# The down projection of a SwiGLU block as one level of Strassen for 18 of its 22 chunks

## The chip, the cores and the metric

The kernel runs on one core of a Trainium2 chip. The metric is device time in microseconds (us), from the start of an execution to its end on that core. The engines are named as the profile names them: PE (TensorE matmuls), PEld (TensorE weight loads), DVE (VectorE), ACT (ScalarE), POOL (GpSimd), and SP (SyncE, which here only issues DMAs). Each engine works through its own list of instructions in order, and waits on semaphores where it needs another engine's result.

## The reference

One transformer block on 1024 tokens of width 1024 in float32: sliding-window attention with sinks, then a SwiGLU feed-forward of inner width 2816 = 22 chunks of 128, then a final norm. The part that the change touches is the last product of the feed-forward:

```python
def swiglu_ffn(h, w_gate_up, w_down):
    gu = h @ w_gate_up
    return (jax.nn.silu(gu[..., :D_FF]) * gu[..., D_FF:]) @ w_down

x = x + mix
x = x + swiglu_ffn(rms_norm(x, norm_ffn), w_gate_up, w_down)
return rms_norm(x, final_norm)
```

## The kernel before

Every float32 operand of a large product is split into a high part (rounded to the matmul's type fp32r, made by ACT) and a low part (operand minus high part, made by DVE or POOL). A product is three matmuls per 128-deep step: high by high, high by low, low by high. All matmuls of the two last stages have 512 columns.

**Gate and up stage** (line 1022). Each of 22 column groups `g` is already done as one level of Strassen: seven products of 12 matmuls in the order 1, 6, 5, 7, 2, 4, 3, with weight sums made by POOL (tile `sum`, line 894), splits into `ws` (ACT line 914, DVE line 918), and evictions from the PSUM banks `gu_A` to `gu_D` on DVE and ACT. A pair of groups gives two chunks of the activation, `gate` times `up` (line 960 on POOL or 962 on DVE), and each finished chunk is stored to DRAM (`act_dram`, line 965).

**Down stage** (line 1219). The 22 chunks are taken in seven rounds of 3, 3, 4, 3, 3, 3, 3. In each round, for each of eight token tiles `t` and two column halves `nh`, PE accumulates the round's chunks in one PSUM bank `d`, and DVE adds the bank to the output tile `acc` in SBUF (line 1227). Activation chunks (`raw_a`) and rows of `w_down` (`raw_d`) come back from DRAM and are split by `d_steps` (ACT line 1122, DVE line 1126) into seven chunk slots of four tiles each; those in the tile `HH`, which held the normed tokens, and in `ws_d` and `dx` are slots of this kind.

The order of all work is written out by hand: `Q.put(n, step)` lets a step be issued after n more matmuls, so that the steps of the next round stand between the matmuls of this one on the other engines' lists.

```python
for t in range(NT):
    for nh in range(2):
        for c in cs:
            for a, b in ((0, 0), (0, 1), (1, 0)):
                nc.tensor.matmul(v4(ps), a_[:, a, t // 2], d_[:, b], ...)
                Q.tick()
        Q.put(4, add)      # acc[t][:, s] = ps + acc[t][:, s], on DVE
```

Of the kernel before, what the change touches and what calls it, by code (L numbers as in the profile page):

```python
# [26 lines left out]
NF = FF // P  # L27
# [5 lines left out]
def trunk_kernel(  # L33
# [13 lines left out]
    nc = tc.nc  # L47
# [47 lines left out]
    class Norm:  # L95
# [468 lines left out]
    def v4(ap):  # L564
        return ap.rearrange("p (k n) -> p k n", k=4)
# [204 lines left out]
    def add_raw_act(c):  # L770
        raw_jobs.append((("a", c), lambda raw: nc.sync.dma_start(raw, act_dram[c])))

    def add_raw_dn(c):
        raw_jobs.append((("d", c), lambda raw: nc.sync.dma_start(raw, w_dn[c * P : (c + 1) * P, :])))
# [330 lines left out]
    slots = {}

    def h_slot(par, k0):
        return [HH[:, j, :, k0 : k0 + 4, par * P : par * P + P] for j in range(4)]

    slots[1], slots[2], slots[4], slots[5] = h_slot(0, 0), h_slot(0, 4), h_slot(1, 0), h_slot(1, 4)  # L1110

    def d_steps(c, j):

        key = ("a" if j < 2 else "d", c)

        def src():
            return v4(raws[key][:, (j % 2) * 512 : (j % 2) * 512 + 512])
# [19 lines left out]
    def d_prep(left):
        for c, j in D_FIRST[left]:
            for i, st in enumerate(d_steps(c, j)):
                Q.put(1 + 3 * i, st)  # L1140
# [60 lines left out]
    c0 = 0  # L1201
    for r, size in enumerate(ROUNDS):
        cs = range(c0, c0 + size)
        c0 += size
        if r + 1 < len(ROUNDS):
            more = [st for c in range(c0, c0 + ROUNDS[r + 1]) for j in range(4) for st in d_steps(c, j)]
            for i, st in enumerate(more):
                Q.put(1 + i * (48 * size - 8) // len(more), st)
        for t in range(NT):
            for nh in range(2):  # L1210
                pool, tag = (psg, "g") if nh else (psa, "a")
                ps = pool.tile([P, 512], F32, tag=tag, name=f"d_{r}_{t}_{nh}")
                s = slice(nh * 512, nh * 512 + 512)
                n = 0
                for c in cs:
                    sl = slots[c % 7]
                    a_, d_ = sl[t % 2], sl[2 + nh]
                    for a, b in ((0, 0), (0, 1), (1, 0)):
                        nc.tensor.matmul(  # L1219
                            v4(ps), a_[:, a, t // 2], d_[:, b],  # L1220
                            start=(n == 0), stop=(n == 3 * size - 1),
                        )
                        n += 1
                        Q.tick()

                def add(r=r, t=t, nh=nh, s=s, ps=ps):
                    nc.vector.tensor_tensor(acc[t][:, s], ps, acc[t][:, s], ALU.add)  # L1227
                    if r == len(ROUNDS) - 1:
                        final_norm(t, nh)

                if t == NT - 1 and r == len(ROUNDS) - 1:
                    add()
                else:
                    Q.put(4, add)
# [30 lines left out]
```

## Time and profile before

| what | value |
|---|---|
| time, median of 3 runs | 1059.92 us (1058.37 to 1060.86) |
| time of the profiled execution | 1059.88 us |
| its span, first to last instruction | 1058.1 us, mean granted TensorE clock 0.985 |
| PE busy | 1026.3 us of the span, 97% |
| DVE, ACT, POOL busy | 609.3, 422.2 and 359.7 us |
| down stage, 808.6 to 1051.0 us | PE busy all of it, 1056 matmuls |

The profile is one execution. Its time is 0.04 us from the median, so that what is worked out from its rows can be set against either. Busy time says how much an engine did, not what the end waits for; for that the chain that ended last is read, and, for one stage, the windows and the waits.

### The profile page before, as it was taken

Reading aid. Unit: us, or ns where it says so; the run is one execution under the profiler, and the core shown is the slowest. Engines: PE = TensorE matmul, PEld = TensorE weight load, DVE = VectorE, ACT = ScalarE, POOL = GpSimd, SP = SyncE. Lnnn points to the kernel's source line nnn. Section 1 sums busy time; section 2 is a strip of 40 time slices with the busy share of each in tenths; the row PEclk is TensorE's granted clock in tenths of the full one; section 3 lists DMA queues with packets and bytes.
Section 4 is the critical chain, followed back from the end, with each engine's and each line's share of the span. In section 5 each row is a group of like instructions: output and inputs, shape, how many; then the busy total and the mean of one; then the engine's idle time right before and its main releaser. Section 6 shows DMA issues by size and latency. Waiting matters only on the chain.

```text
span 1058.1 us, 13677 instructions
## 1 busy us (share of the span) xinstructions
PE 1026.3 (97%) x4848; PEld 846.1 (80%) x4848; DVE 609.3 (58%) x1071; ACT 422.2 (40%) x893; POOL 359.7 (34%) x406
## 2 busy tenths in 40 slices
PE   7999999999987899999999999999999999999997
PEld 7888788888765698888888888888888888888885
DVE  5421687778885666454555455456446664455545
ACT  5432777777754443322332332232333212221115
POOL 4634555565334454163254154245131000000001
PEclk8999999999988899999999999999999999999999
DMA  8457555554546423132122132132126632233103
GB/s 276 127 132 204 138 160 146 154 179 130 141 125 190 132 80 100 60 106 73 60 100 99 41 120 77 44 120 80 42 99 237 239 121 80 80 100 99 42 20 139
DMA packets 92500, 124.11 MB, mean 117 GB/s; under 512 B 5648, under 2 KB 66064, under 8 KB 92432
## 3 DMA queue, kind: packets, MB, share of 16 engines
q1 hardware_dynamic: 92144, 122.45, 37.5%
q8 instruction: 38, 0.62, 0.2%
q10 hardware_dynamic: 288, 0.79, 0.2%
q14 instruction: 30, 0.25, 0.1%
HBM read 92.81 MB, written 28.31 MB: 114 GB/s over the span
## 4 chain that ended last, share of the span: by engine, by line
PE 64%; POOL 1%; ACT 1%; DVE 0%; issue 0%; POOLq 0%; ACTq 0%
PE d L1219 23%; PE gu_C L1022 12%; PE gu_B L1022 12%; PE gu_A L1022 12%; PE gu_D L1022 6%; PE mo L1035 1%; POOL sum L894 0%; POOL wc_oB L63 0%; POOL xr L636 0%; ACT acc L1197 0%; DVE ws L918 0%; PE pt_b L615 0%; ACT junk L1181 0%; ACT HT L616 0%; ACT sq L1174 0%
## 5 line engine op out<-in xcount | busy, mean ns | idle before, releaser
L1219 PE MATMUL d<-HH 128*128 128x512 f32 x576 | 150.6, 393 | 0.0
L1227 DVE TENSOR_TENSOR acc<-d,acc 128x512 f32<-128x512 f32 x112 | 77.3, 691 | 110.1 <-PE d L1219 103.8
L1022 PE MATMUL gu_A<-HH,ws 128*128 128x512 f32 (+2 forms) x552 | 132.2, 388 | 0.0
L960 POOL TENSOR_TENSOR gate<-gate,up 128x512 f32<-128x512 f32 x33 | 47.6, 1443 | 246.3 <-issue 195.0
L1219 PEld LDWEIGHTS d<-HH 128*128 128x128 f32 x576 | 108.3, 188 | 23.8
L246 PE MATMUL pc<-HH,wc_c 128*128 128x512 f32 x480 | 122.0, 398 | 0.0
L1022 PEld LDWEIGHTS gu_A<-HH,ws 128*128 128x128 f32 x552 | 101.7, 188 | 22.9
L918 DVE TENSOR_TENSOR ws<-sum,ws 128x512 fp32r<-128x512 f32 x88 | 85.9, 987 | 54.8 <-ACT ws L914 54.2
L246 PEld LDWEIGHTS pc<-HH,wc_c 128*128 128x128 f32 x480 | 87.4, 188 | 17.8
L914 ACT ACTIVATE ws<-raw_g 128x512 fp32r<-128x512 f32 x66 | 40.9, 630 | 140.0 <-issue 51.4
L1219 PE MATMUL d<-ws_d,ws_d 128*128 128x512 f32 x336 | 94.9, 391 | 0.0
L914 ACT ACTIVATE ws<-sum 128x512 fp32r<-128x512 f32 x88 | 54.0, 626 | 99.8 <-POOL sum L894 62.8
L1175 POOL TENSOR_SCALAR ssq_f<-ssq_f 128x1 f32<-128x1 f32 x7 | 1.3, 191 | 232.7 <-ACT sq L1174 232.7
L491 POOL TENSOR_SCALAR t<-t,st 128x256 f32<-128x256 f32 (+1 forms) x128 | 60.4, 491 | 52.8 <-DVE st L489 34.9
L1219 PEld LDWEIGHTS d<-ws_d,ws_d 128*128 128x128 f32 x336 | 63.0, 188 | 14.3
L478 ACT ACTIVATE t<-t,st 128x256 f32<-128x256 f32 (+1 forms) x128 | 61.9, 485 | 29.1 <-DVE st L470 29.1
L918 DVE TENSOR_TENSOR ws<-raw_g,ws 128x512 fp32r<-128x512 f32 x66 | 56.0, 857 | 29.7 <-ACT ws L914 28.8
L1022 PE MATMUL gu_C<-HT,ws 128*128 128x512 f32 (+2 forms) x288 | 67.6, 382 | 0.4 <-DVE ws L918 0.4
L979 DVE TENSOR_TENSOR u<-gu_B,p 128x512 f32<-128x512 f32 x44 | 30.3, 689 | 65.1 <-PE gu_B L1022 57.1
L1022 PE MATMUL gu_D<-HT,ws 128*128 128x512 f32 (+2 forms) x276 | 66.4, 389 | 0.0
L1022 PE MATMUL gu_B<-HT,ws 128*128 128x512 f32 (+2 forms) x276 | 65.9, 388 | 0.0
L1022 PE MATMUL gu_C<-HH,ws 128*128 128x512 f32 x264 | 65.2, 396 | 0.0
(165 smaller groups left out, 1871.9 us busy)
## 6 DMA issues: line engine op xcount, KB each, us to landing
raw_g<-in_ffn_w_gate_up_dram SPq DMA_DIRECT2D x44, 512.0 KB, 3.6
act<-gate SPq DMA_DIRECT2D x22, 512.0 KB, 2.6
raw_a<-act SPq DMA_DIRECT2D x22, 512.0 KB, 3.3
raw_d<-in_ffn_w_down_dram SPq DMA_DIRECT2D x22, 512.0 KB, 3.3
raw_c<-in_swa_w_in_dram SPq DMA_DIRECT2D x20, 512.0 KB, 4.0
qs<-qst SPq DMA_DIRECT2D x64, 128.0 KB, 2.5
qt<-qs SPq DMA_DIRECT2D x32, 256.0 KB, 4.6
x<-in_x_dram SPq DMA_DIRECT2D x8, 512.0 KB, 5.8
```

Of the source, the lines that this page charges most:

```text
L246: nc.tensor.matmul(ps, wc[:, wl, k], hh[:, :, hl, k, :], start=(n == 0), stop=(n == 3 * NK - 1))
L478: nc.scalar.activation(self.tt[:, g, b0:], self.tt[:, g, b0:], AF.Exp, bias=st[:, 0, g : g + 1], scale=-1.0, accum_out=st[:, 3, g : g + 1],)
L491: nc.gpsimd.tensor_scalar(self.tt[:, g, b0:], self.tt[:, g, b0:], st[:, 2, g : g + 1], 0.0, ALU.mult, ALU.add)
L914: nc.scalar.activation(w[:, 0], src(), AF.Copy)
L918: nc.vector.tensor_tensor(w[:, 1], src(), f(w[:, 0]), ALU.subtract)
L960: nc.gpsimd.tensor_tensor(gate[:, s], gate[:, s], ups[kp, f_][:, s], ALU.mult)
L979: nc.vector.tensor_tensor(us[g][:, n * 512 : n * 512 + 512], banks[g, "B"], p1s[g], ALU.add)
L1022: nc.tensor.matmul(v4(ps)[:, j0:j1], w[:, wl, k], moving(i, hl, k, j0, j1), start=(first and part != "l" and n == 0), stop=(n == 11), skip ...
L1035: nc.tensor.matmul(opss[2 * i + nh], o[:, a, c % G], wt[:, b, c % 2], start=(c == 0 and n == 0), stop=(c == 7 and n == 2),)
L1175: nc.gpsimd.tensor_scalar(st[:, 3:4], st[:, 0:1], 1.0 / D, EPS, ALU.mult, ALU.add)
L1219: nc.tensor.matmul(v4(ps), a_[:, a, t // 2], d_[:, b], start=(n == 0), stop=(n == 3 * size - 1),)
L1227: nc.vector.tensor_tensor(acc[t][:, s], ps, acc[t][:, s], ALU.add)
```

## The change

It replaces the down stage for 18 of the 22 chunks. Two neighbouring chunks of the activation (a pair `p`, nine pairs) times two column halves of `w_down`, with even and odd token tiles as the other split, are one 2 by 2 block product, and it is done with seven block products instead of eight. The nine pairs go in four rounds of 2, 2, 2 and 3 (`DROUNDS`). In a round, product `i` in the order 1, 2, 6, 7, 5, 3, 4 (`DORDER`) runs over `j` = 0 to 3 (each `j` is a pair of token tiles) and over the pairs, 3 matmuls each: 24 matmuls in a round of two pairs, 36 in the round of three. Products 1, 2 and then 5, 3 share the four banks X; 6, 7 and then 4 the four banks Y: product 2 adds on the banks of product 1 after product 1's own value was taken out, and likewise 7 on 6 and 3 on 5. The last four chunks are done as before, all at the end, 12 matmuls for each tile and half.

The left operands (sums of activations) are made in the gate and up stage by POOL, four for each pair (`act_sums`), and stored as three and a half tiles a pair in place of two. The right operands (differences of blocks of `w_down`) are made by POOL in the down stage, in `d_steps`, four for each pair: two for product 6, one for 7, one for 4. Both are split as before, the left ones (`s`) by ACT and POOL, the right ones (`w`) by ACT and DVE, into a ring of 16 slots, all in `HH`. Evictions stay on DVE, but for products 1 and 7 of the first round, which ACT copies. Four output tiles get their last sums on POOL (`y_sums`).

```diff
+    DROUNDS = (2, 2, 2, 3)
+        elif acts[kp, f_] == 2 and acts.get((kp, 1 - f_), 0) == 2:
+            act_sums(kp)
...
+            (u1[:, a], g0[:, b], g1[:, b], ALU.add),
+            (u0[:, b], g0[:, a], g0[:, b], ALU.subtract),
+            (u0[:, a], u1[:, a], g0[:, a], ALU.subtract),
+            (u1[:, b], g1[:, a], u0[:, a], ALU.subtract),
+        )):
+            Q.put(2 + 5 * i, lambda dst=dst, x_=x_, y_=y_, op=op: nc.gpsimd.tensor_tensor(dst, x_, y_, op))
...
+    DORDER = (1, 2, 6, 7, 5, 3, 4)
+    for o, op in enumerate(dops):
+        d_slot[op] = slots[o % 16]
...
+            if i == 6:
+                steps = [tt(b11, b12, b11), t2]
+            elif i == 7:
+                steps = [tt(b12, b22, b12)]
+            elif i == 4:
+                steps = [lambda: tt(b21, b21, t2_raw[p])()]
         def hi():
+            nc.scalar.activation(dst[:, 0], v4(src()), AF.Copy)
         def lo():
+            eng.tensor_tensor(dst[:, 1], v4(src()), f(dst[:, 0]), ALU.subtract)
+        return steps + [hi, lo]
...
+    def d_more(n, spread):
+            free = (NG - 1, (1, 7, 2, 3)[o // 4]) in done if o < 16 else dops[o - 16][1:] in d_done
...
+    def d_product(r, i):
+        first = i in (1, 6, 5, 4)
+        bank = "X" if i in (1, 2, 5, 3) else "Y"
+        for j in range(4):
+            for p in ps_:
+                a_, d_ = d_slot["s", i, p], d_slot["w", i, p]
+                for a, b in ((0, 0), (0, 1), (1, 0)):
+                    nc.tensor.matmul(
+                        v4(ps), a_[:, a, j], d_[:, b], start=(first and n == 0), stop=(n == 3 * len(ps_) - 1),
...
+                if r == 0 and i in (1, 7):
+                    nc.scalar.activation(dst, ps, AF.Copy)
+                else:
+                    nc.vector.tensor_tensor(dst, ps, dst, ALU.add)
+            Q.put(3, out_)
...
-    ROUNDS = (3, 3, 4, 3, 3, 3, 3)
+    for r, ps_ in enumerate(drounds):
+        for i in DORDER:
+            w_more()
+            d_more(2 * len(ps_) + 1, 12 * len(ps_) - 3)
+            d_product(r, i)
+            for p in ps_:
+                d_done.add((i, p))
```

On PE, in the down stage before, a bank's matmuls stand together, and only the bank's first waits for PE's own semaphore or for a slot (bank `d_1_2_0` is round 1, tile 2, half 0):

```order
L1219 MATMUL d_1_2_0_7263<-ws2_d_3_2_7028,ws2_d_3_0_6995 128x512 [waits PE_49]
L1219 MATMUL d_1_2_0_7263<-ws2_d_3_2_7028,ws2_d_3_0_6995 128x512 x2
L1219 MATMUL d_1_2_0_7263<-HH_77 128x512 x6
L1219 MATMUL d_1_2_1_7276<-ws2_d_3_2_7028,ws2_d_3_0_6995 128x512 [waits PE_49]
L1219 MATMUL d_1_2_1_7276<-ws2_d_3_2_7028,ws2_d_3_0_6995 128x512 x2
L1219 MATMUL d_1_2_1_7276<-HH_77 128x512 x6
```

On PE now, in round 1, these rows are products 1 (its last two `j`) and 2; a bank `d_1_1_2` is round 1, the product that opened it (1), `j` = 2:

```order
L1305 MATMUL d_1_1_2_7412<-HH_77 128x512 [waits DVE_49]
L1305 MATMUL d_1_1_2_7412<-HH_77 128x512 x5
L1305 MATMUL d_1_1_3_7425<-HH_77 128x512 [waits DVE_49]
L1305 MATMUL d_1_1_3_7425<-HH_77 128x512 x5
L1305 MATMUL d_1_1_0_7388<-HH_77 128x512 [waits DVE_49,Activation_49]
...
L1305 MATMUL d_1_1_1_7401<-HH_77 128x512 [waits DVE_49]
L1305 MATMUL d_1_1_1_7401<-HH_77 128x512 x5
L1305 MATMUL d_1_1_2_7412<-HH_77 128x512 [waits DVE_49]
L1305 MATMUL d_1_1_2_7412<-HH_77 128x512 x5
```

Each bank of product 1 comes a second time, for product 2, 24 matmuls after its first; each time its first matmul waits for DVE.

On POOL, in the down stage before, nothing but one-column steps of the final norm stands behind the last product of the gate and up stage:

```order
L960 TENSOR_TENSOR gate_10_1_6779<-gate_10_1_6779,up_10_1_6911 128x512 [waits DVE_49,Activation_49]
L960 TENSOR_TENSOR gate_10_0_6797<-gate_10_0_6797,up_10_0_6960 128x512 [waits DMAHW5_49,DVE_49,Activation_49]
L1175 TENSOR_SCALAR ssq_f_0_8333<-ssq_f_0_8333 128x1 [waits Activation_49]
L1176 TENSOR_TENSOR ssq_f_0_8333<-ssq_f_0_8333,small_76 128x1 [waits Pool_49]
L1175 TENSOR_SCALAR ssq_f_1_8360<-ssq_f_1_8360 128x1 [waits Activation_49]
```

On POOL now, in round 1, this is all that it does while PE runs product 4 of round 0 and product 1 of round 1 (lows of the left operands of products 6 and 7, `raw_s_2_1` and `raw_s_3_1` for pairs 2 and 3, and the differences of `w_down` rows, `wd2` and `t2`):

```order
L1235 TENSOR_TENSOR HH_77<-raw_s_2_1_7198,HH_77 128x4x128 [waits PE_49,DMAHW3_49,Activation_49,Pool_49]
L1212 TENSOR_TENSOR wd2_4_6975<-wd2_4_6975 128x512 [waits DMAHW5_49,DVE_49]
L1216 TENSOR_TENSOR t2_2_7353<-wd2_4_6975 128x512 [waits DMAHW6_49,Pool_49]
L1235 TENSOR_TENSOR HH_77<-raw_s_3_1_7221,HH_77 128x4x128 [waits DMAHW4_49,PE_49,Activation_49]
L1212 TENSOR_TENSOR wd2_6_7020<-wd2_6_7020 128x512 [waits DMAHW1_49,DVE_49]
L1216 TENSOR_TENSOR t2_3_7374<-wd2_6_7020 128x512 [waits Pool_49]
L1235 TENSOR_TENSOR HH_77<-raw_s_2_1_7198,HH_77 128x4x128 [waits PE_49,Activation_49]
L1212 TENSOR_TENSOR wd2_4_6975<-wd2_4_6975 128x512
L1235 TENSOR_TENSOR HH_77<-raw_s_3_1_7221,HH_77 128x4x128 [waits PE_49,Activation_49]
L1212 TENSOR_TENSOR wd2_6_7020<-wd2_6_7020 128x512
```

Ten full instructions came to an engine that had none there, six for product 6 and four for product 7.

On DVE, in the down stage before, splits and evictions alternate, and a split takes its source from DRAM by way of ACT alone:

```order
L1126 TENSOR_TENSOR HH_77<-raw_a_9_7253,HH_77 128x4x128 [waits DMAHW6_49,Activation_49]
L1227 TENSOR_TENSOR acc_5_6976<-d_1_5_1_7363,acc_5_6976 128x512 [waits DVE_49,PE_49]
L1126 TENSOR_TENSOR HH_77<-raw_a_9_7253,HH_77 128x4x128 [waits Activation_49]
L1227 TENSOR_TENSOR acc_6_6977<-d_1_6_0_7376,acc_6_6977 128x512 [waits DVE_49,PE_49]
L1126 TENSOR_TENSOR HH_77<-raw_d_9_7280,HH_77 128x4x128 [waits DMAHW7_49,Activation_49]
```

On DVE now, at the same place as the rows of POOL (evictions of product 4, then of product 1 into `y1`, with the lows of the right operands of products 6 and 7):

```order
L1235 TENSOR_TENSOR HH_77<-t2_2_7353,HH_77 128x4x128 [waits Activation_49]
L1316 TENSOR_TENSOR acc_1_7063<-d_0_4_0_7342,acc_1_7063 128x512 [waits PE_49]
L1316 TENSOR_TENSOR acc_3_7065<-d_0_4_1_7355,acc_3_7065 128x512 [waits PE_49]
L1235 TENSOR_TENSOR HH_77<-t2_3_7374,HH_77 128x4x128 [waits Activation_49]
L1316 TENSOR_TENSOR acc_5_7067<-d_0_4_2_7366,acc_5_7067 128x512 [waits PE_49]
L1316 TENSOR_TENSOR acc_7_7069<-d_0_4_3_7379,acc_7_7069 128x512 [waits PE_49]
L1235 TENSOR_TENSOR HH_77<-wd2_4_6975,HH_77 128x4x128 [waits Activation_49]
L1316 TENSOR_TENSOR y1_0_7070<-d_1_1_0_7388,y1_0_7070 128x512 [waits PE_49]
L1316 TENSOR_TENSOR y1_1_7071<-d_1_1_1_7401,y1_1_7071 128x512 [waits PE_49]
L1235 TENSOR_TENSOR HH_77<-wd2_6_7020,HH_77 128x4x128 [waits Activation_49]
L1316 TENSOR_TENSOR y1_2_7072<-d_1_1_2_7412,y1_2_7072 128x512 [waits PE_49]
L1316 TENSOR_TENSOR y1_3_7073<-d_1_1_3_7425,y1_3_7073 128x512 [waits PE_49]
```

The evictions of product 1 now stand behind lows whose source is made by POOL and then rounded by ACT.

## Rows read from the trace of the kernel before

**Rows 1.** Page, part 1: busy us (share of the span) and instructions of each engine.

```profile
PE 1026.3 (97%) x4848; PEld 846.1 (80%) x4848; DVE 609.3 (58%) x1071; ACT 422.2 (40%) x893; POOL 359.7 (34%) x406
```

**Rows 2.** Page, part 4: the chain that ended last, shares by engine and line.

```profile
PE d L1219 23%; PE gu_C L1022 12%; PE gu_B L1022 12%; PE gu_A L1022 12%; PE gu_D L1022 6%; PE mo L1035 1%; POOL sum L894 0%; POOL wc_oB L63 0%; POOL xr L636 0%; ACT acc L1197 0%; DVE ws L918 0%; PE pt_b L615 0%; ACT junk L1181 0%; ACT HT L616 0%; ACT sq L1174 0%
```

**Rows 3.** Windows: us, busy PE, PEld, DVE, ACT, POOL, clock, DMA share, GB/s.

```profile
420.00:800.00 380.00, 380.00 (x1630) 306.13 (x1630) 192.09 (x242) 115.85 (x199) 145.06 (x102) 1.00 0.25 81
808.60:1051.00 242.40, 242.40 (x1057) 198.12 (x1055) 132.34 (x198) 55.27 (x94) 7.00 (x16) 1.00 0.32 111
1051.00:1058.10 7.10, 0.07 (x1) 0.00 (x0) 2.25 (x4) 2.55 (x4) 0.81 (x2) 0.67 0.53 214
```

**Rows 4.** Timeline of PE in gate and up: start, us, group of matmuls.

```profile
702.16 2.96 PE L1022 MATMUL gu_A<-HH,ws 128*128 128x512 f32 x12
704.96 2.96 PE L1022 MATMUL gu_D<-HT,ws 128*128 128x512 f32 x12
```

**Rows 5.** Line 1219: duration ns min/median/max, first and last start of its matmuls.

```profile
L1219 PE MATMUL d<-HH x576: 388/393/398, 809.3 to 1049.3; 128*128 128x512 f32 x192
L1219 PE MATMUL d<-ws_d,ws_d x336: 386/391/397, 808.6 to 1050.7; 128*128 128x512 f32 x168
L1219 PE MATMUL d<-dx,dx x144: 388/390/398, 874.7 to 1050.0; 128*128 128x512 f32 x144
```

**Rows 6.** Waits in the down stage: us in total, times, longest.

```profile
DVE acc L1227 <- PE d L1219: 103.8, 103, 2.1
ACT HH L1122 <- DMA raw_d<-in_ffn_w_down_dram: 47.3, 9, 13.6
```

**Rows 7.** Timeline of ACT in gate and up, behind the PE group of [rows 4].

```profile
705.22 0.63 ACT L914 ACTIVATE ws<-raw_g 128x512 fp32r<-128x512 f32 x1 [0.27 <-PE gu_A L1022]
705.75 0.62 ACT L914 ACTIVATE ws<-sum 128x512 fp32r<-128x512 f32 x1
```

**Rows 8.** Timeline of ACT and POOL in the attention stage.

```profile
208.66 1.05 ACT L60 ACTIVATE wc_o<-raw_o 128x1024 fp32r<-128x1024 f32 x1
209.80 2.40 POOL L63 TENSOR_TENSOR wc_o<-raw_o,wc_o 128x1024 fp32r<-128x1024 f32 x1 [0.41 <-ACT wc_o L60]
```

**Rows 9.** Timeline of POOL, ACT and DVE around one burst of POOL.

```profile
607.11 1.29 POOL L960 TENSOR_TENSOR gate<-gate,up 128x512 f32<-128x512 f32 x1 [21.84 <-issue]
613.35 1.30 POOL L894 TENSOR_TENSOR sum<-raw_g,raw_g 128x512 f32<-128x512 f32 x1
614.72 1.29 POOL L894 TENSOR_TENSOR sum<-sum,raw_g 128x512 f32<-128x512 f32 x1
616.05 0.63 ACT L914 ACTIVATE ws<-sum 128x512 fp32r<-128x512 f32 x1 [5.21 <-POOL sum L894]
616.71 1.10 DVE L918 TENSOR_TENSOR ws<-sum,ws 128x512 fp32r<-128x512 f32 x1 [3.26 <-ACT ws L914]
617.22 1.75 POOL L894 TENSOR_TENSOR sum<-raw_g 128x512 f32<-128x512 f32 x1
619.02 3.45 DVE L918 TENSOR_TENSOR ws<-sum,ws 128x512 fp32r<-128x512 f32 x2
```

**Rows 10.** Timeline of PE and DVE in the down stage.

```profile
843.71 0.85 PE L1219 MATMUL d<-ws_d,ws_d 128*128 128x512 f32 x3
843.91 0.69 DVE L1227 TENSOR_TENSOR acc<-d,acc 128x512 f32<-128x512 f32 x1 [0.17 <-PE d L1219]
844.52 0.68 DVE L1126 TENSOR_TENSOR dx<-raw_d,dx 128x512 fp32r<-128x512 f32 x1
```

**Rows 11.** Windows at two pauses of PE before gate and up, columns as in [rows 3].

```profile
338.00:343.00 5.00, 1.39 (x9) 0.88 (x8) 2.05 (x3) 1.54 (x2) 0.06 (x1) 1.00 1.03 323
343.00:347.00 4.00, 4.00 (x15) 3.32 (x16) 4.00 (x6) 1.20 (x2) 0.00 (x0) 0.57 1.01 337
361.00:364.00 3.00, 0.95 (x3) 0.19 (x2) 1.86 (x3) 2.15 (x4) 2.27 (x1) 0.99 0.00 0
364.00:368.00 4.00, 3.86 (x10) 3.08 (x11) 3.64 (x6) 2.08 (x5) 0.20 (x2) 0.58 0.02 9
```

More of the change, by code (lines that the diff above doesn't have):

```diff
@@ L79, in trunk_kernel @@
     x2_dram = [dram.tile([P, D], F32, name=f"x2s_{t}") for t in range(NT)]
-    act_dram = [dram.tile([P, T], F32, name=f"act_{c}") for c in range(NF)]
+    DROUNDS = (2, 2, 2, 3)
+    NPAIR = sum(DROUNDS)
+    actp_dram = [[dram.tile([P, T], F32, name=f"actp_{p}_{b}") for b in range(4)] for p in range(NPAIR)]
+    act_dram = {c: dram.tile([P, T], F32, name=f"act_{c}") for c in range(2 * NPAIR, NF)}
     def hslot(t):
@@ L768, in add_raw_gu, with add_raw_act @@
         raw_jobs.append((("g", g, kh), go))
[L770 to L774, printed above, removed]
+    def add_raw_act(key, src, n=T):
+        raw_jobs.append((key, lambda raw: nc.sync.dma_start(raw[:, :n], src[:, :n])))
     NG = NF
@@ L779, in trunk_kernel @@
         add_raw_gu(g, 1)
-    for c in range(NF):
-        add_raw_act(c)
-        add_raw_dn(c)
+    drounds = []
+    for n in DROUNDS:
+        at_ = drounds[-1][-1] + 1 if drounds else 0
+        drounds.append(range(at_, at_ + n))
+        for b in range(4):
+            for p in drounds[-1]:
+                add_raw_act(("s", p, b), actp_dram[p][b], 512 if b == 3 else T)
+    for c in act_dram:
+        add_raw_act(("a", c), act_dram[c])
     s2 = Stream(out0_steps())
@@ L1102, in trunk_kernel @@
         at(w, n_both, 3, b)
[L1105 to L1117, printed above, removed]
+    slots = [HH[:, j, :, k0 : k0 + 4, par * P : par * P + P] for par, k0 in ((0, 0), (1, 0), (0, 4), (1, 4)) for j in range(4)]
@@ new lines, in trunk_kernel, with w_free, w_more @@
+    G_OPS = len(seq)
+    def w_free(a):
+        m = a % 9
+        olds = (a - 9,) if m < 3 else (a - 9, a - 8) if m % 2 else ()
+        return all(seq[o] in done if o < G_OPS else o - G_OPS in w_closed for o in olds)
+    def w_more():
+        nonlocal w_next, w_pair
+        while w_next < NF and w_free(G_OPS + w_next):
+            c, m = w_next, (G_OPS + w_next) % 9
+            if m < 3:
+                raw = wp.tile([P, 1024], F32, tag="raw", name=f"wd_{c}", bufs=3)
+            elif m % 2:
+                w_pair = wp.tile([P, 2, 1024], F32, tag="wc", name=f"wd2_{c}", bufs=3)
+                raw = w_pair[:, 0]
+            else:
+                raw = w_pair[:, 1]
+            nc.sync.dma_start(raw, w_dn[c * P : (c + 1) * P, :])
+            w_raw[c] = raw
+            w_next += 1
@@ L1137, in d_prep @@
[L1137 to L1140, printed above, removed]
+            eng.tensor_tensor(dst[:, 1], v4(src()), f(dst[:, 0]), ALU.subtract)
+            if end:
+                end()
+                w_more()
+        return steps + [hi, lo]
+    def d_more(n, spread):
+        nonlocal ndop
+        todo = []
+        while n and ndop < len(dops):
+            o = ndop
+            free = (NG - 1, (1, 7, 2, 3)[o // 4]) in done if o < 16 else dops[o - 16][1:] in d_done
+            steps = d_steps(dops[o]) if free else None
+            if steps is None:
+                break
+            todo.append(steps)
+            ndop += 1
+            n -= 1
+        total = sum(len(st) for st in todo)
+        for k, st in enumerate(st for steps in todo for st in steps):
+            Q.put(1 + k * spread // total, st)
@@ L1149, in trunk_kernel @@
             after(*item[1:])
-        left = len(head) - 1 - n
-        if left < 7:
-            d_prep(left)
+        if len(head) - 1 - n < 7:
+            w_more()
+            d_more(2, 10)
     Q.flush()
@@ L1198, in final_store @@
         nc.sync.dma_start(out[t * P : (t + 1) * P, :], acc[t])
-    ROUNDS = (3, 3, 4, 3, 3, 3, 3)
[L1201 to L1234, printed above, removed]
@@ new lines, in trunk_kernel, with y_sums @@
+    for r, ps_ in enumerate(drounds):
+        for i in DORDER:
+            w_more()
+            d_more(2 * len(ps_) + 1, 12 * len(ps_) - 3)
+            d_product(r, i)
+            for p in ps_:
+                d_done.add((i, p))
+    def y_sums(j):
+        a, b = slice(0, 512), slice(512, 1024)
+        lo, up = acc[2 * j], acc[2 * j + 1]
+        return [
+            lambda dst=dst, x_=x_: nc.gpsimd.tensor_tensor(dst, dst, x_, ALU.add)
+            for dst, x_ in ((lo[:, b], y1[j]), (y7[j], y1[j]), (up[:, a], y7[j]), (up[:, b], y7[j]))
+        ]
@@ new lines, in trunk_kernel, with add @@
+    for j in range(4):
+        for k, st in enumerate(y_sums(j)):
+            Q.put(6 + 22 * j + 5 * k, st)
+    while ndop < len(dops):
+        w_more()
+        before = ndop
+        d_more(16, 4)
+        Q.tick()
+        assert ndop > before
+    for t in range(NT):
+        for nh in range(2):
+            pool, tag = (psg, "g") if nh else (psa, "a")
+            ps = pool.tile([P, 512], F32, tag=tag, name=f"dl_{t}_{nh}")
+            s = slice(nh * 512, nh * 512 + 512)
+            n = 0
+            for c in LAST4:
+                a_, d_ = d_slot["c", c, t % 2], d_slot["c", c, 2 + nh]
+                for a, b in ((0, 0), (0, 1), (1, 0)):
+                    nc.tensor.matmul(v4(ps), a_[:, a, t // 2], d_[:, b], start=(n == 0), stop=(n == 11))
+                    n += 1
+                    Q.tick()
+            def add(t=t, nh=nh, s=s, ps=ps):
+                nc.vector.tensor_tensor(acc[t][:, s], ps, acc[t][:, s], ALU.add)
+                final_norm(t, nh)
+            if t == NT - 1:
+                add()
+            else:
+                Q.put(4, add)
```

104 lines of the change are left out of this document (88 added, 16 removed).

## The prediction

> **What bounds the kernel now.** The page first: PE is busy for 97% of the span [rows 1], and the chain that ended last runs over PE's lines alone, 23% of it on the down stage's line 1219 [rows 2]. The windows then show the two stages that the change touches: PE has no idle time in 380 us of gate and up, nor in the 242.4 us of the down stage, at full clock in both [rows 3]. So a matmul removed there is time gained, and a wait of PE is time lost. The down stage's other engines have room: POOL 7.0 us, ACT 55.3, DVE 132.3 of 242.4 [rows 3]. The waits there are DVE's for PE and ACT's for transfers [rows 6], and none is PE's.
>
> **What is removed.** 1056 matmuls start between 808.6 and 1050.7 us [rows 5]: 242.1 / 1055 = 0.2295 us each. Now there are 4 x 7 x 3 x 9 = 756 for the pairs and 16 x 12 = 192 for the four chunks, 948: 108 fewer, **-24.8 us**. In gate and up the same kind of matmul takes 2.80 / 12 = 0.2333 us [rows 4]. If that pace came along, the gain would be 242.1 - 221.2 = 20.9 us. I take 0.2295, since the operands and their slots are the down stage's.
>
> **What costs nothing.** The left sums are 36 POOL instructions, 1.37 us apart as in [rows 9]: 49 us on an engine that is busy for 145 of 380 us [rows 3] and idle for 21.8 us ahead of the burst beside which they stand [rows 9]. Without that cover a pair's four would hold up the weight sums behind them by 5.5 us. The stores and reloads grow by one and a half tiles of 0.5 MB a pair each way, some 14 MB in all, on DMA engines busy to 25 to 32% [rows 3]. The last stage has its 16 operand tiles in the ring, and the tail after the last matmul, 7.1 us [rows 3], is unchanged code.
>
> **What is added to the path.** In the new down stage PE waits for DVE wherever one product adds on the banks of the one before: product 2's bank may be written only when DVE has taken out product 1's value. The lists show DVE's evictions of product 1 behind the lows of product 7's right operand, whose source POOL makes and ACT rounds. What one step costs: an ACT rounding 0.63, the next one 0.53 later, and 0.26 from PE's next group to ACT's start [rows 4, 7]; ACT to POOL 0.09 [rows 8]; a POOL instruction 1.30, the next 1.37 after it, POOL to ACT 0.04, ACT to DVE 0.03 [rows 9]; a low 0.68, an eviction 0.69, 0.20 behind PE [rows 10].
>
> Follow round 1, with PE's start of product 4 of round 0 as zero; a product of 24 matmuls lasts 5.5 us, so product 1 starts at 5.5 and product 2 is due at 11.0. ACT rounds the left tile of product 6's first pair when product 3's slots are free, 0.3 to 0.9. POOL: its low, two differences, 1.0 to 5.0. ACT: the difference 5.1 to 5.7, the second pair's left tile to 6.2. POOL again three, 6.3 to 10.35. ACT: second difference to 11.0, product 7's left tile to 11.55. POOL: low and difference, 11.6 to 14.3. ACT to 15.0. DVE: product 7's first right low to 15.7, and only then the evictions of product 1: `j` = 0 to 16.3, 1 to 17.0. The second pair takes the same way: POOL 15.6 to 18.3, ACT to 18.9, DVE to 19.7, evictions of `j` = 2 to 20.3 and of 3 to 21.0. PE starts product 2 at 16.35 in place of 11.0 (5.3 lost), does two banks (2.75), and waits again from 19.1 to 20.3 (1.2): **6.5 us**. What is late next is nothing: by product 6 DVE has caught up. The same happens in round 2.
>
> Round 0 has the burst across the border: six POOL instructions of product 6 and two products of `gate` and `up` stand ahead of product 7's four, and ACT's copies of product 1 stand behind them. From POOL's free time, 5.2 us ahead of the border, the same prices put the first copy at 11.1 where PE wants it at 5.5, and a second wait of 1.5: **7.0**. In the round of three, a product lasts 8.3 us; product 6's first two pairs fit, its third and product 7's three come as ten POOL instructions, and product 7's third right low ends at 28.9 us after product 1's start. The evictions of product 6 are behind it; product 7 is due at 24.8 and starts at 29.6: **4.8**. Product 4, one difference a pair, does the same in small: last low at 9.0, and product 3 gets its bank 0.7 late (1.4 in round 0): **2.8** over three rounds. Waits in all 7.0 + 2 x 6.5 + 4.8 + 2.8 = **27.6 us**.
>
> The bounds of this sum: POOL does 1024 columns in 2.40 [rows 8], so 1.20 for 512 is the low end; a long burst has about ten POOL steps in its chain, a short one four, and 0.1 less takes 4 x 1.0 + 3 x 0.4 = 5.2 us off: 22.4. At the high end a POOL instruction takes 1.75 beside a DVE instruction that reads SBUF twice, and two such lows 3.45 [rows 9]. I take 1.30, since in the chain DVE mostly waits while POOL works.
>
> **The clock.** A pause of PE of this length has a row: after the mostly idle 5 us from 338 the clock is 0.57 over the next 4 us, and so it is after that from 361 [rows 11], that is the lower of its two levels, 1.2 of 2.4 GHz, for most of the stretch; it costs 4.0 x (1 - 0.57) = 1.7 us of matmuls each time. In rounds 1 and 2 product 2's second wait takes up 1.2 of it, in round 0 all; in round 3 nothing does: 0.5 + 0.5 + 1.7 = **2.7**, from 0 to 6.8 at most. The Trainium skill (TensorE: Matmul & The Clock Gate, Part 1) says that the clock falls after an idle stretch and comes back with sustained work. By that rule each long wait costs something like this; the rows agree with it.
>
> **The sum.** -24.8 + 27.6 + 2.7 = +5.5 us on 1059.88, the profiled execution's own time, which is 0.04 from the median: **1065.4 us**, slower by 0.5%.
>
> **Rivals.** *No wait reaches PE (faster).* Place: product 2's first bank. It decides whether DVE has evicted product 1's `j` = 0 within 11.0 us of product 4's start, where I have 16.3. For it: the operands themselves are made three products ahead, and POOL has almost nothing to do in this stage now. Against it: the lists are in order on all three engines, and today ACT already waits 5.2 us for POOL and DVE 3.3 for ACT in such a burst [rows 9], where only other banks save PE. All 24.8 gained: 1035. A half-way case, in which the waits come to 10 to 20 us without the clock's share, gives 1045 to 1055.
>
> *POOL and DVE hold each other up (much slower).* A low beside POOL's work costs POOL 1.75 - 1.30 = 0.45 and DVE up to 1.1 [rows 9]. A round of two pairs has 22 POOL instructions and 14 DVE lows, 22 x 1.30 + 14 x 0.68 = 38.1 us in 7 x 5.5 = 38.5 us of matmuls; if half of the 14 lengthen a POOL step of a chain, 3.2 a round, and with the clock's 6.8 the time is 1065.4 + 12.8 + 4.1 = 1082. For it: the rows of the burst. Against it: in the chain above the lows fall into POOL's pauses, and evictions read PSUM. The Trainium skill (SBUF — State Buffer, Who interferes with whom) has it as a lock: a DVE instruction with two SBUF inputs and a GpSimd instruction that reads SBUF exclude each other for the whole of the instruction. By that rule the two engines' 38.1 us would be one queue and this rival the likeliest; in the rows the loss is 0.45 of POOL's 1.30, less than a full block.
>
> *The left sums hold up gate and up.* 5.5 us at nine pairs if nothing covers them, 49 us; against it, POOL's 235 idle us there and PE without a wait [rows 3, 9]. Two or three us at most.
>
> **How the numbers follow.** Less than 0.2%, 2.1 us, can hardly be told from no change here. Chances: waits as worked out, 1058 to 1074, 0.55; port rival, 1074 to 1084, 0.13; half-way case, 1042 to 1058, 0.18; no wait at all, 0.11; left sums 0.03. Faster: 0.11, most of the half-way case, 0.16, and the low edge of the first, 0.04, make 0.31. Within 0.2%: 0.13, all from the first case's low part and the half-way case's end. Slower: 0.56. The range goes from 1043 to 1079: it leaves out the case without waits and the far end of the port rival. The likeliest case's own range is 1058 to 1074.
>
> **What would show it.** Right: 756 and 192 matmuls at 0.23 us; PE idle in the down stage for some 28 us, in four pieces of 5 us and more ahead of product 2 (rounds 0 to 2) and of product 7 (round 3), released by DVE's line 1316 (ACT's 1314 in round 0); DVE idle ahead of its lows (line 1235) for ACT, ACT for POOL; clock below 1 behind each. Wrong: PE without idle time there; POOL's instructions at 1.0 or 1.75; a wait of PE in gate and up; or PE held by a transfer at the border, where 4 MB of `acc` go ahead of other loads.

## The result, and the profile after

The changed kernel takes **1066.67 us** (median of 4 runs, 1065.65 to 1066.94), the one before in the same session 1059.74 (4 runs): ratio 1.0064, 95% interval 1.0047 to 1.0082. It is 0.6% slower. The profiled execution took 1066.94 us, its span is 1065.1.

The page's first part, against [rows 1]: the matmuls are 108 fewer, PE is busy for 19.1 us less, and yet the span is 7.0 longer. POOL has 151 instructions more.

```profile
PE 1007.2 (95%) x4740; PEld 828.8 (78%) x4740; DVE 617.8 (58%) x1070; ACT 454.6 (43%) x955; POOL 573.4 (54%) x557
```

The windows, with the columns of [rows 3] and the stages' new borders: the down stage begins at 817.1 in place of 808.6 and its matmuls end at about 1057.5.

```profile
420.00:800.00 380.00, 373.03 (x1587) 298.69 (x1586) 190.69 (x235) 110.00 (x189) 194.00 (x137) 1.00 0.30 102
817.10:1057.50 240.40, 222.50 (x948) 181.90 (x947) 142.62 (x203) 93.72 (x164) 161.73 (x126) 0.96 0.38 134
1057.50:1065.10 7.60, 0.44 (x2) 0.01 (x1) 2.12 (x4) 2.34 (x4) 0.82 (x2) 0.77 0.40 155
...
```

Two things differ from before. In gate and up, where PE had no idle time, 7.0 us are now missing; the clock there is 1.00 in the mean, though 0.50 from 505.2 to 508.6 us, behind the first pause. And the down stage, with a tenth fewer matmuls, is only 2.0 us shorter (240.4 against 242.4). The waits of PE from 400 us on (us in total, times, longest):

```profile
PE d L1305 <- DVE y L1316: 8.1, 2, 4.0
PE d L1305 <- ACT y L1314: 6.4, 1, 6.4
PE gu_B L1054 <- DVE u L1011: 6.0, 3, 2.1
PE d L1305 <- DVE acc L1316: 3.4, 2, 3.2
PE gu_C L1054 <- DVE gate L1015: 0.9, 1, 0.9
```

Three lines are the forecast waits of the down stage: ACT's copy in round 0, DVE's evictions of product 1 in rounds 1 and 2, of product 6 in round 3. The two `gu` lines were not forecast. Taken from the start times of the matmuls (a gap less the usual step of 0.23 us), the down stage loses 6.55 + 0.37 in round 0, 0.38 ahead of its product 3, 4.20 + 0.34 in round 1, 4.19 in round 2 and 3.38 + 0.34 in round 3, together **19.75 us**; gate and up loses 2.25, 1.06, 2.25 and 2.03 at 502, 632, 664 and 706 us, together **7.6**. The 0.37 and the two 0.34 are not waits: each is the step from the first matmul behind a pause to the second, at a granted clock of 0.50, and the list above has no second wait in these rounds. So of the 19.75 us 18.7 are waits, and 1.05 belong to the clock.

The timeline of the down stage around round 1's wait (start us, us, instruction, idle time ahead of it and what ended it), with the rows of other operands left out:

```profile
859.00 1.30 POOL L1235 TENSOR_TENSOR HH<-raw_s,HH 128x512 fp32r<-128x512 f32 x1 [2.47 <-ACT HH L1232]
...
866.80 1.29 POOL L1216 TENSOR_TENSOR t<-wd 128x512 f32<-128x512 f32 x1
868.12 0.63 ACT L1232 ACTIVATE HH<-t 128x512 fp32r<-128x512 f32 x1 [4.03 <-POOL t L1216]
868.66 0.62 ACT L1232 ACTIVATE HH<-raw_s 128x512 fp32r<-128x512 f32 x1
...
869.35 1.27 POOL L1235 TENSOR_TENSOR HH<-raw_s,HH 128x512 fp32r<-128x512 f32 x1 [1.27 <-ACT HH L1232]
...
870.59 1.26 POOL L1212 TENSOR_TENSOR wd<-wd 128x512 f32<-128x512 f32 x1
871.88 0.63 ACT L1232 ACTIVATE HH<-wd 128x512 fp32r<-128x512 f32 x1 [2.60 <-POOL wd L1212]
...
872.54 0.69 DVE L1235 TENSOR_TENSOR HH<-wd,HH 128x512 fp32r<-128x512 f32 x1 [1.86 <-ACT HH L1232]
...
873.15 1.28 DVE L1316 TENSOR_TENSOR y<-d,y 128x512 f32<-128x512 f32 x2
873.98 3.83 PE L1305 MATMUL d<-HH 128*128 128x512 f32 x9 [4.04 <-DVE y L1316]
```

Read from below: PE waits for `y`, the eviction of product 1; `y` stands behind the low of product 7's right operand, which waits for ACT's rounding, which waits for POOL's difference (`wd`). POOL itself had to wait for ACT's rounding of the left tile, which stood behind a rounding that waited for POOL. All three engines are idle in turn.

In gate and up the same kind of chain appears, with the left sums (line 989) in it. POOL, ACT, DVE and PE ahead of the first pause:

```profile
495.00 1.29 POOL L967 TENSOR_TENSOR gate<-gate,up 128x512 f32<-128x512 f32 x1 [1.28 <-DVE up L1015]
496.37 1.29 POOL L989 TENSOR_TENSOR up<-gate,gate 128x512 f32<-128x512 f32 x1
...
497.62 1.30 POOL L901 TENSOR_TENSOR sum<-raw_g,raw_g 128x512 f32<-128x512 f32 x1
498.87 1.30 POOL L989 TENSOR_TENSOR up<-gate 128x512 f32<-128x512 f32 x1
498.94 0.63 ACT L921 ACTIVATE ws<-sum 128x512 fp32r<-128x512 f32 x1 [6.59 <-POOL sum L901]
...
500.12 1.74 POOL L901 TENSOR_TENSOR sum<-sum,raw_g 128x512 f32<-128x512 f32 x1
...
501.90 0.63 ACT L921 ACTIVATE ws<-sum 128x512 fp32r<-128x512 f32 x1 [1.84 <-POOL sum L901]
...
502.56 1.08 DVE L925 TENSOR_TENSOR ws<-sum,ws 128x512 fp32r<-128x512 f32 x1 [1.85 <-ACT ws L921]
...
503.57 0.68 DVE L1011 TENSOR_TENSOR u<-gu_B,p 128x512 f32<-128x512 f32 x1
...
504.40 2.21 PE L1054 MATMUL gu_B<-HH,ws 128*128 128x512 f32 x6 [2.09 <-DVE u L1011]
```

Left sums and weight sums alternate on POOL. Two left sums, 2.6 us, stand ahead of the second weight sum; ACT and DVE wait for that, the eviction `u` stands behind DVE's low, and PE's product 7 needs `u`. Further on, POOL is idle for 17.7 us (512.5 to 530.2).

### The profile page after: what moved, and what is told of

It reads as the page before. It is cut to its first block, busy times and chain, and to the rows that moved or that the text cites. A ratio compares the mean times of both kernels' runs of the same rounds, so it can differ in the third digit from the quotient of the medians.

```text
span 1065.1 us, 13843 instructions
## 1 busy us (share of the span) xinstructions
PE 1007.2 (95%) x4740; PEld 828.8 (78%) x4740; DVE 617.8 (58%) x1070; ACT 454.6 (43%) x955; POOL 573.4 (54%) x557
## 5 line engine op out<-in xcount | busy, mean ns | idle before, releaser
L1305 PE MATMUL d<-HH 128*128 128x512 f32 x756 | 179.4, 400 | 17.9 <-DVE y L1316 8.1
L1305 PEld LDWEIGHTS d<-HH 128*128 128x128 f32 x756 | 146.1, 194 | 51.1 <-ACT HH L1232 13.1
L925 DVE TENSOR_TENSOR ws<-sum,ws 128x512 fp32r<-128x512 f32 x88 | 81.2, 932 | 92.8 <-ACT ws L921 92.5
L1235 POOL TENSOR_TENSOR HH<-raw_s,HH 128x512 fp32r<-128x512 f32 x63 | 90.8, 1456 | 74.9 <-ACT HH L1232 66.1
L1235 DVE TENSOR_TENSOR HH<-wd,HH 128x512 fp32r<-128x512 f32 x62 | 51.3, 831 | 50.9 <-ACT HH L1232 50.9
L925 DVE TENSOR_TENSOR ws<-raw_g,ws 128x512 fp32r<-128x512 f32 x66 | 65.5, 1002 | 23.6 <-ACT ws L921 22.9
L1054 PE MATMUL gu_B<-HH,ws 128*128 128x512 f32 x264 | 67.0, 403 | 6.0 <-DVE u L1011 6.0
L63 POOL TENSOR_TENSOR wc_c<-raw_c,wc_c 128x1024 fp32r<-128x1024 f32 x20 | 48.0, 2402 | 34.9 <-ACT wc_c L60 34.6
L1054 PEld LDWEIGHTS gu_B<-HH,ws 128*128 128x128 f32 x264 | 50.5, 192 | 19.3 <-issue 7.3
```

The costliest lines, as they stand in the source:

```text
L63: lo_eng.tensor_tensor(lo, src, f(hi), ALU.subtract)
L1054: nc.tensor.matmul(v4(ps)[:, j0:j1], w[:, wl, k], moving(i, hl, k, j0, j1), start=(first and part != "l" and n == 0), stop=(n == 11), skip ...
L1235: eng.tensor_tensor(dst[:, 1], v4(src()), f(dst[:, 0]), ALU.subtract)
L1305: nc.tensor.matmul(v4(ps), a_[:, a, j], d_[:, b], start=(first and n == 0), stop=(n == 3 * len(ps_) - 1), skip_group_check=True,)
```

## The experiments

In every one the kernel before ran on the same chip. Its medians were 1058.58 us (beside no_right, no_left, late7 and pool_plus), 1057.74 (late7b, late_left, alternate and both) and 1058.27 (the three of experiment 7), where it had 1059.74 beside the changed kernel; so the ratios are the better measure between kernels. Losses by gaps are taken as above, from the profile, which is one execution.

**1. Without the right differences (no_right).**

```diff
-            if i == 6:
-                steps = [tt(b11, b12, b11), t2]
-            elif i == 7:
-                steps = [tt(b12, b22, b12)]
-            elif i == 4:
-                steps = [lambda: tt(b21, b21, t2_raw[p])()]
...
-                1: lambda: b11, 2: lambda: b21, 6: lambda: t2_raw[p], 7: lambda: b12, 5: lambda: b11,
+                1: lambda: b11, 2: lambda: b21, 6: lambda: b22, 7: lambda: b12, 5: lambda: b11,
```

> The differences of the right operands are left out: products 6, 7, 5 and 4 round raw blocks of the weights (36 POOL instructions less; the output is not the reference's). Everything else stays. Theory (in the down stage DVE's evictions stand behind lows that wait for ACT, which waits for these POOL instructions): the 19.7 us of pauses in the down stage go, and with them the half-clock stretches behind them (some 8.5 us): 1066.7 - 28.2 = 1038, and the four pauses in gate and up (7.6 us) stay. Rival (POOL and DVE hold each other up, or the 14 lows a round and the evictions are too much for DVE anyway): at most half goes, 1052 or more. Rival (transfers of the left sums or the weights come late): no change, 1065 to 1068.

1039.64 us, ratio 0.9831 (0.9814 to 0.9847). The down stage has no gap and full clock, with ACT's and DVE's work and all transfers still in place; the window of its matmuls:

```profile
815.00:1029.50 214.50, 214.50 (x948) 177.60 (x947) 155.95 (x202) 91.26 (x161) 117.06 (x91) 1.00 0.42 150
```

The 7.6 us in gate and up stay. So without the POOL differences no wait of the down stage is left, and the larger transfers cost nothing there.

**2. Without the left sums (no_left).**

```diff
-            Q.put(2 + 5 * i, lambda dst=dst, x_=x_, y_=y_, op=op: nc.gpsimd.tensor_tensor(dst, x_, y_, op))
+            pass
...
-            nc.sync.dma_start(rows_[1], u0)
-            nc.sync.dma_start(rows_[2], u1)
+            nc.sync.dma_start(rows_[1], g0)
+            nc.sync.dma_start(rows_[2], g1)
```

> The left sums are left out: the 36 POOL instructions of line 989 are gone and the stores write the gate tiles in their place, with the same bytes (the output is not the reference's). Theory (the left sums stand among the weight sums in POOL's list, so that ACT, DVE and then PE wait in gate and up): the pauses of 7.6 us between 500 and 710 us go, and one half-clock stretch (1.7 us): 1066.7 - 9.3 = 1057.4, the first matmul of the down stage at 808 in place of 817, the down stage as before. Rival (the pauses come from the stores, or from the multiplications on POOL that were there before): no change, 1065 to 1068.

1057.07 us, ratio 0.9985 (0.9972 to 0.9998). No gap in gate and up, first matmul of the down stage at 808.8 us, gaps of 19.3 us behind it. The left sums, not their stores, make the pauses.

**3. Product 7's rounding and lows one product later (late7, then late7b).**

```diff
+            if late and dops[o][:2] == ("w", 7) and dops[o][2] < 6:
+                for k, st in enumerate(steps[1:]):
+                    Q.put(late + 4 + 10 * (dops[o][2] % 2) + 4 * k, st)
+                steps = steps[:1]
...
-            d_more(2 * len(ps_) + 1, 12 * len(ps_) - 3)
+            d_more(2 * len(ps_) + 1, 12 * len(ps_) - 3, 24 if r < 3 else 0)
```

This is late7b; late7 did the same for the pairs of round 3 as well. In both the raw tile is given back only when both its readers, products 7 and 5, have been issued.

> The same work on the same engines, but the rounding and the low of product 7's right operands are issued one product later, so that product 1's evictions stand ahead of these lows in DVE's list; POOL's list stays. Theory (what counts is the place in DVE's list): the waits of rounds 1 and 2 fall from 4.2 to about 1.1 (product 6's last low still stands ahead), that of round 0 from 6.6 to between 0 and 2, that of round 3 (3.4) stays: some 12 us less, and 3 to 5 of the clock's: 1049 to 1052. Rivals (POOL is too slow for its share, or DVE and POOL hold each other up): the work is the same, so the wait only moves to product 7: 1064 to 1069.

late7: 1048.75 us, ratio 0.9912 (0.9897 to 0.9927); gaps of 3.0, 0.3, 0.6, 1.6 and 1.6 us, none in round 3. But in its round 3 the lows are issued behind the matmuls that use them, which therefore work on stale operands; that round, and with it the time, is no measure of the change. late7b is.

> The later place of product 7's rounding and lows in rounds 0 to 2 alone; round 3 is as in the changed kernel. (In the run before, round 3's lows fell behind the matmuls that use them, so that its round 3 used stale operands.) Theory: rounds 0 to 2 as in that run (gaps of about 3.0, 1.6 and 1.6 us), round 3's wait of 3.4 us and its half-clock stretch come back: 1048.75 + 3.4 + 1.2 = 1053.4. Rival (the place in DVE's list does not matter): 1064 to 1069.

late7b: 1054.65 us, ratio 0.9973 (0.9963 to 0.9984). The profile is of the fastest of its ten executions, 1051.11 us. Its waits of PE in the down stage:

```profile
PE d L1316 <- DVE acc L1327: 3.6, 2, 3.2
PE d L1316 <- DVE y L1327: 2.9, 2, 1.5
PE d L1316 <- ACT y L1325: 2.7, 1, 2.7
```

DVE's 8.1 us of `y` waits are 2.9, ACT's 6.4 are 2.7, and round 3's 3.2 is as it was. Nothing was taken off an engine: the same instructions, further down in ACT's and DVE's lists, save 9.6 us of gaps. Behind round 3's gap the clock did not fall in the profiled execution.

**4. One more POOL instruction ahead of each difference of product 7 (pool_plus).**

```diff
-                steps = [tt(b12, b22, b12)]
+                steps = [lambda: nc.gpsimd.tensor_tensor(spare(p), b22, b12, ALU.subtract), tt(b12, b22, b12)]
```

> One more POOL instruction of the same kind ahead of each difference of product 7 (9 in all, into a spare tile that nothing reads). Theory: each of them stands in the chain POOL, ACT, DVE low, eviction, PE: the first wait of rounds 0 to 2 grows by 1.3 us, the second by as much again, and the wait of round 3 by 3 x 1.3 = 3.9: 3 x 2.6 + 3.9 = 11.7, 1078. Rival (the waits are set by something else, by transfers, DVE's own work or ACT's): 9 instructions of 1.3 us on an engine that is busy half of the time change nothing, 1065 to 1068.

1079.03 us, ratio 1.0197 (1.0175 to 1.0219), 12.4 above the changed kernel by the medians and 14 by the ratios. The waits, in the fastest of its executions (1076.37 us):

```profile
PE d L1309 <- DVE y L1320: 11.0, 3, 5.4
PE d L1309 <- ACT y L1318: 8.8, 2, 7.7
PE d L1309 <- DVE acc L1320: 7.3, 1, 7.3
```

The longest grow from 4.0 to 5.4, from 6.4 to 7.7 and from 3.2 to 7.3: one POOL step of 1.3 us in rounds 0 to 2, three in round 3. The second waits, forecast to grow by as much, are 1.1 us in round 0 and 0.2 in round 1: there PE took 4.7 us for the two banks ahead of it, most of it at half clock, in place of 2.7 at full clock, and so reached the next bank later.

**5. The left sums 70 ticks later (late_left).**

```diff
-            Q.put(2 + 5 * i, lambda dst=dst, x_=x_, y_=y_, op=op: nc.gpsimd.tensor_tensor(dst, x_, y_, op))
+            Q.put(72 + 6 * i, lambda dst=dst, x_=x_, y_=y_, op=op: nc.gpsimd.tensor_tensor(dst, x_, y_, op))
...
-        Q.put(30, store)
+        Q.put(100, store)
```

> All left sums are computed, but issued 70 ticks (16 us) later, where POOL was idle for 17.7 us between the weight sums; the stores come later by as much. Theory (what costs is the place among the weight sums, not POOL's 49 us of work): the four pauses in gate and up go, as when the sums were left out: 1057. Rival (POOL's added work, or its traffic beside DVE, costs wherever it stands): 1062 to 1068.

1057.36 us, ratio 0.9997 (0.9985 to 1.0009), as without the sums. Gate and up, with all its POOL work:

```profile
420.00:800.00 380.00, 380.00 (x1630) 305.94 (x1629) 205.37 (x241) 114.97 (x197) 201.42 (x140) 1.00 0.31 105
```

PE is busy for all 380 us while POOL works for 201: only the place of the sums had cost.

**6. Another order of products (alternate), and with the later left sums (both).**

```diff
-    DORDER = (1, 2, 6, 7, 5, 3, 4)
+    DORDER = (1, 6, 2, 7, 5, 4, 3)
...
-            b, h = {1: (0, 0), 2: (0, 1), 6: (1, 0), 7: (1, 1), 5: (2, 0), 3: (2, 1), 4: (3, 0)}[i]
+            b, h = {1: (0, 0), 6: (0, 1), 2: (1, 0), 7: (1, 1), 5: (2, 0), 4: (2, 1), 3: (3, 0)}[i]
...
-        bank = "X" if i in (1, 2, 5, 3) else "Y"
+        bank = "X" if (i in (1, 2, 5, 3)) == (r % 2 == 0) else "Y"
```

> The same products in the order 1, 6, 2, 7, 5, 4, 3, with the banks of the two groups swapped in every second round, so that no product adds on the banks of the one right before it; the halves of the stored left rows change places to match. An eviction then has a whole product (5.5 or 8.3 us) more. Theory: every wait in the down stage was shorter than that (6.6 at most, 4.2 and 3.4 otherwise), so 0 to 1 us of 19.75 is left, and the clock's 5.8 go too: 1066.7 - 25.5 = 1041, as when the differences were left out. Rival (a late low holds PE itself, now that product 6 is needed one product earlier): 1050 or more.

1052.52 us, ratio 0.9951 (0.9936 to 0.9966): a miss. The clock stays at full, but gaps of 7.4 us are left in the down stage, five of 0.9 to 1.7 us and smaller ones, and 26 steps of 0.3 to 0.5 us lose 3.4 more. The time is the rival's, its cause only in part: PE is held by a late low for 1.0 us, and by evictions for 5.2 (DVE's `acc` 2.4, `up` at the border 1.5, ACT's copy 1.3). What is left can be read in DVE's timeline of the run with both edits:

> The new order of products and the later left sums together. Theory: the two losses are in different stages and add up: 1041 - 9.2 = 1032 (1029 to 1035), that is 0.974 of the kernel before, with no pause of PE over 1 us behind 400 us. Rival (the left sums' later place takes from POOL what the new order needs, or one of the two only moves its wait): 1040 or more.

1041.94 us, ratio 0.9849 (0.983 to 0.9867), as far above its forecast as the first.

```profile
852.22 0.69 DVE L1237 TENSOR_TENSOR HH<-t,HH 128x512 fp32r<-128x512 f32 x1 [3.27 <-ACT HH L1234]
852.83 1.28 DVE L1318 TENSOR_TENSOR acc<-d,acc 128x512 f32<-128x512 f32 x2
```

PE takes up its next product at 853.57, 0.97 late, behind this `acc`. It is the same wait with another operand: product 6 now is needed one product earlier, so its second low (`t`) stands ahead of the evictions in place of product 7's. The order alone moves the chain to other operands; POOL's steps are as many.

**7. The lows of two left operands on DVE (s67_dve, s67_late, both_s67).**

```diff
-            eng = nc.gpsimd
+            eng = nc.vector if i in (6, 7) else nc.gpsimd
```

> The changed kernel with the lows of the left operands of products 6 and 7 on DVE in place of POOL (18 instructions of 1.30 us become 18 of 0.68); all else as in the changed kernel. Theory (POOL's steps in the chain set the wait, 1.3 us each): ahead of product 7's first right low four POOL lows of the chain go in rounds 1 and 2, so that its waits of 4.2 go to nothing; round 0's falls from 6.6 to some 2, round 3's from 3.4 to nothing; the clock's 5.8 go too: 1066.7 - 17.7 - 5.8 = 1043. Rival (DVE is what is late, its own lows and evictions): 9 to 18 more lows in front of the evictions, 1055 or more.

1045.67 us, ratio 0.989 (0.9877 to 0.9904). Rounds 1 to 3 have no gap over 0.3 us; of round 0's 6.6 us 3.1 are left. So the differences alone do not make the waits of rounds 1 to 3: it takes the lows of the left operands between them in POOL's list.

> The same with the left sums 70 ticks later in gate and up. Theory: 9.2 less than the run before, 1034, with the products in the order of the changed kernel, so that the new order is not needed. Rival: as for the run before, 1046 or more.

1036.46 us, ratio 0.98 (0.9787 to 0.9813).

> New order of products, later left sums, and the lows of the left operands of products 6 and 7 on DVE. Theory: what was left of waits with the first two (6.3 us in rounds 0 to 3, behind the difference of product 6's second pair) shrinks to 3 or less: 1041.9 - 3.5 = 1038.5. Rival (what was left is DVE's own lateness): 1042 to 1046.

1030.16 us, ratio 0.9735 (0.9722 to 0.9749): 2.65% faster than the kernel before, and better than forecast. Its trace has no wait of PE between 400 us and the last matmul. The windows:

```profile
420.00:800.00 380.00, 380.00 (x1631) 305.90 (x1630) 203.97 (x239) 114.45 (x196) 203.50 (x141) 1.00 0.33 105
807.20:1021.80 214.60, 214.60 (x948) 177.70 (x947) 166.04 (x221) 93.79 (x165) 147.85 (x108) 1.00 0.42 150
```

DVE is busier than in the changed kernel, 166.0 us in 214.6, and is never late. This speaks against DVE's own load as the cause of what was left in experiment 6.

## Why the prediction was right about the time, and where it was not

The forecast was 1065.4 us, and 1066.67 came; slower was the likeliest side. But two steps were off, in opposite directions: the down stage was forecast 5.5 us longer and is 1.7 shorter by its matmuls' starts, and gate and up, forecast unchanged, is 8.5 longer. That the total came within 1.3 us is luck: with the down stage alone the kernel would have been no slower than before. By terms, forecast and measured:

| term, us | forecast | measured | from |
|---|---|---|---|
| fewer matmuls | -24.8 | -27.2 | 948 x 0.2270 - 1056 x 0.2295 |
| waits in the down stage | +27.6 | +18.7 | gaps ahead of a first matmul, less 0.23 each |
| clock in the down stage | +2.7 | +6.8 | 5.8 from intervals of 0.3 to 0.5 us, less 0.227 each, and the 1.05 above |
| gate and up (left sums) | 0 | +8.5 | first matmul of `d` at 817.1, before 808.6 |
| sum | +5.5 | +6.8 | spans: 1065.1 - 1058.1 = 7.0 |

- *The removed matmuls*: right in count. The pace was mis-sized: 0.2270 us in the down stage's undisturbed stretches where I kept 0.2295, worth 2.4 us. What makes a matmul of the same shape 2.5 ns shorter was not tried.
- *The waits*: the mechanism was right in place, releaser and order, round by round, and experiments 1, 3 and 4 show it from three sides. The size was too large. Of round 1's 6.5 us 4.2 came: product 7's first low starts 13.6 us after product 4's first matmul where I had 15.0, as POOL began 0.9 earlier than I put it; and the second wait (1.2) did not come, because PE, at half clock, took 4.4 us for the two banks ahead of it where I had 2.75. Round 0 was 6.55 in one wait (forecast 7.0 in two), round 2 4.2 (6.5), round 3 3.4 (4.8). Product 4's small bursts were forecast at 2.8; only one of 0.38 came. The price of a POOL step, 1.30, held: pool_plus adds 1.3 for each in the chain.
- *The clock*: the sign was right, the size 6.8 for 2.7. I let the second waits take up the loss; it was the other way round, the loss took up the second waits. Both together were forecast at 30.3 and measured at 25.5.
- *What costs nothing*: **this step failed**. I set 49 us of left sums against POOL's 235 idle us in the stage and against one place with 21.8 idle us ahead of a burst. I did not look at which instructions they would stand between. They are issued right behind the multiplications, while the weight sums of a burst are being issued, and delayed them in four places; the text had the price, 5.5 us a pair without cover, and gave that case a chance of 0.03 at "two or three us at most". Experiment 2 shows that they cost it, and experiment 5 that it is their place. Why four of nine pairs pause and the others not was not followed up. The larger transfers cost nothing, as forecast (experiment 1).
- *The rivals*: no wait at all and the half-way case did not happen. That POOL and DVE hold each other up does not set the time: experiment 7 gave DVE 18 more lows with two SBUF inputs and took as many instructions from POOL, and gained 21 us over the changed kernel by the medians, some 18 by the ratios. The Trainium skill (SBUF — State Buffer, Who interferes with whom) has a DVE instruction with two SBUF inputs and a reading GpSimd instruction exclude each other. By that rule the lows would still wait on POOL here. The rows of the changed kernel agree with it, and "less than a full block" was a misreading: the one that starts first keeps its undisturbed time, and the other is longer by about what was left of the first. In the 31 places of its trace behind 370 us where just one POOL instruction and one low overlap, the two together last 1.82 to 1.96 us, where one behind the other would be 1.30 + 0.69 = 1.99. Two of them, one with POOL first and one with DVE:

```profile
552.68 1.30 POOL L901 TENSOR_TENSOR sum<-raw_g 128x512 f32<-128x512 f32 x1
552.73 1.79 DVE L925 TENSOR_TENSOR ws<-raw_g,ws 128x512 fp32r<-128x512 f32 x1 [1.22 <-ACT ws L921]
...
534.92 0.69 DVE L925 TENSOR_TENSOR ws<-raw_g,ws 128x512 fp32r<-128x512 f32 x1
535.05 1.72 POOL L967 TENSOR_TENSOR gate<-gate,up 128x512 f32<-128x512 f32 x1 [2.34 <-DVE up L1015]
```

POOL's 0.45 in [rows 9] was set against its own 1.30, but a low of 0.68 can take no more than 0.68 from it. In the chain of round 1 this costs next to nothing, since one engine works while the other waits (lows of 0.69 on DVE, 1.26 to 1.30 on POOL). In the first pause of gate and up it is an estimated 0.8 of the 2.25 us: POOL's second weight sum took 1.74 and DVE's low behind it 1.08, where 1.30 and 0.69 are undisturbed.

## What to carry to other kernels

Idle time summed over a stage does not cover added work; ask which instructions it will stand between, and who waits for the next one in that list. Issuing the same 36 sums 16 us later took their cost from 8.5 us to nothing. Where a result passes through three engines in order, anything queued behind it pays for the slowest link: put evictions that PE needs ahead of it in the list, or move one link to another engine, and look again, since a new order can put the next operand in the same place.

## What the hardware showed that was not expected

The clock's fall does not follow from the length of a pause alone. Behind round 3's gap of 3.6 us in the changed kernel PE ran at the lower of its two levels, 1.2 of 2.4 GHz, and in the profiled execution of late7b, with the same gap of 3.6, it did not. Behind the first pause of gate and up, 2.5 us, it fell in the changed kernel, and in late7 and s67_dve, with the same pause, it did not. The windows behind the four long pauses of the changed kernel's down stage and, last, behind that first one:

```profile
826.10:832.90 6.80, 3.80 (x9) 3.03 (x10) 0.73 (x2) 2.83 (x6) 4.32 (x4) 0.50 1.02 371
873.90:877.30 3.40, 3.32 (x8) 2.68 (x9) 1.53 (x3) 1.66 (x4) 2.14 (x3) 0.50 0.46 155
918.20:921.60 3.40, 3.40 (x9) 2.62 (x8) 1.53 (x4) 2.02 (x4) 2.14 (x3) 0.50 0.47 154
979.70:983.10 3.40, 2.98 (x7) 2.43 (x8) 3.40 (x6) 3.40 (x7) 3.40 (x3) 0.50 0.27 54
...
505.20:508.60 3.40, 3.40 (x10) 2.63 (x9) 1.22 (x2) 0.63 (x1) 3.40 (x3) 0.50 0.59 220
```

There a matmul starts 0.427 us behind the one before, in place of 0.227. The shorter gaps of experiment 6, 1.9 us at most, were followed by full clock throughout the down stage. And the same matmul has a steady pace of 0.2267 to 0.2270 us in every version of the new down stage but the two of experiment 6 (0.2275 at most), against 0.2295 before and 0.2333 in gate and up, at the same granted clock.
